# A decoder layer in one kernel: the second product of its MLP written as seven block products

## The chip, the cores and the metric

The kernel runs on one core of a Trainium2 chip. The core has TensorE (PE in the profile, with its weight loads as PEld), VectorE (DVE), ScalarE (ACT), GpSimd (POOL) and SyncE (SP), which here only starts transfers; 16 DMA engines carry those. The metric is the time of one execution on the device, in microseconds; lower is better. Times before and after are medians of several runs, and one run more is taken with the hardware profiler; the rows of this document are from that one.

## The reference, cut to what matters

One layer, for 1024 tokens of width 1024, all in fp32 (DFF is 4096):

```python
h = rmsnorm(x, norm_mix_g)
u = h @ w_in                                   # then two token mixers and two gates
x = x + merged @ w_out                         # "out_proj" below
h = rmsnorm(x, norm_mlp_g)
x = x + jnp.square(jax.nn.relu(h @ w_ff1)) @ w_ff2      # first and second product of the MLP
gate = jax.nn.sigmoid(rmsnorm(x, norm_ple_g) @ w_ple_gate)
x = x + (p @ w_ple) * gate                     # "gate stage" below
return rmsnorm(x, final_norm_g)
```

w_ff1 is 1024x4096, w_ff2 4096x1024, w_ple_gate 1024x1024.

## The kernel before, in words

**A product.** An fp32 operand is held as two parts of TensorE's faster fp32 type: a high part, which ScalarE casts, and a low part (the operand less its high part), which VectorE or GpSimd subtracts. One product of a 128x128 block with a 128x512 block is then three matmuls, hi·hi, hi·lo and lo·hi (`mm3`, L155 to L160). They accumulate in a bank of PSUM.

**The stages.** After the mixers comes `out_proj` (L882). For each half c of the output columns and each tile j of 128 tokens it makes 24 matmuls. In the second half it also runs `norm(j - 1)` behind tile j: the norm of the token tile, its transposition on TensorE (`pt`), the product with the norm's weights (`h`, L902) and, for odd j, four subtractions that prepare the operands of the MLP's first product (L907). The last tile's norm stands behind the last matmul.

`phase_ff1` (L963) makes the first product in Strassen's form. A 2x2 product of blocks takes eight block products; in this form (Winograd's variant) seven do, of sums of the blocks, and the results are sums of these. Here 16 groups of 2 column tiles of w_ff1 go through the block products ORDER = [0, 5, 1, 6, 4, 3, 2], twelve matmuls each (512 tokens wide). `stationary` (L1005) makes the weights' sums, `moving` (L993) the sums of h and their parts, once, in group 0. As these take time, products 0 and 1 of the first AHEAD = 4 groups, which need neither, are made first. The sums of the results are `u`, `v`, `x` (L1065); `store` applies the squared ReLU (L1031) and writes one 128x512 tile to `dr_hid` in DRAM (L1032), four a group.

`phase_ff2` (L1084) makes the second product in the plain way: eight groups of four rows of hidden blocks; each group loads four hidden blocks (`h0r` to `h3r`, 512 KB each) and four of w_ff2 (`w0r` to `w3r`, L1100), casts them (L952) and makes their low parts (L953), the next group's during the present one's matmuls. Each of the eight token tiles takes 24 matmuls into one tile `p` (two banks), and VectorE adds that to `x2` (L1120), which was read back from DRAM in eight loads `x` (L1110).

`phase_ple` (L1123) is the gate stage: the eight blocks of w_ple_gate are loaded and split (`plg0hi`, `plg0lo` and on; low parts on GpSimd, L1146) during the second product. Each token tile is normed (`xn`; Square on ScalarE, `rs_v`, a power on GpSimd for `rs_r`, then L122), transposed and goes through 48 matmuls for the gate (`pg`), 12 for the embedding (`pw`) and the last norm.

**What sets the order.** A scheduler of the language orders each engine's instructions by their place in the program and their readiness, before the run; on the chip every engine then works through its list in that order and waits at an instruction whose inputs are not there. SP's list holds all transfers, on one queue: a store that waits for its result holds up all the loads behind it. A tile of a pool with `bufs` buffers can be filled only when the use of the one that many before it is done.

Of the kernel before, what the change touches and what calls it, by code (L numbers as in the profile page):

```python
# [79 lines left out]
class Kern:  # L80
    def __init__(self, tc, A, out):
        self.tc, self.nc, self.A, self.out = tc, tc.nc, A, out
        self.raws = {}
# [79 lines left out]
    def run(self):  # L163
        nc, tc, A = self.nc, self.tc, self.A
        with ExitStack() as es:
# [13 lines left out]
            self.dr_hid = dr.tile([DFF // P, P, T], F32, name="dr_hid")  # L179
# [10 lines left out]
            with ExitStack() as right:  # L190
# [3 lines left out]
                self.f1w = opener(mid)("f1w", 5)  # L194
# [687 lines left out]
    def out_proj(self, pool, mA):  # L882
# [9 lines left out]
        def norm(j, xj):  # L892

            xn = self.norm_scale(xj, (nw, nw))
            nc.sync.dma_start(self.dr_x2[j, :, H:D], xj[:, H:D])
            col = lambda c: slice(c * H + j // 2 * P, c * H + (j // 2 + 1) * P)
            blk = lambda kk, c: self.h2[:, 4 * kk:4 * kk + 4, col(c)]
            for q in range(2):
# [4 lines left out]
                if j % 2 == 0:  # L903
                    self.split([t[:, :, col(0)] for t in self.hb[q]], blk(q, 0), q)
            if j % 2:
# [3 lines left out]
                sub(blk(0, 0), blk(0, 1), blk(0, 0))  # L909
                sub(t1, blk(1, 1), blk(0, 0))  # L910
                sub(blk(1, 0), blk(1, 0), t1)
                sub(blk(0, 1), blk(1, 1), blk(0, 1))

        for c in range(2):
            cols = slice(c * H, c * H + H)
            ws = [self.weights(wp, A["w_out"][k][:, cols], [P, H], "wo", lo="gv"[k % 2], raw_bufs=2) for k in range(KD)]
            for j in range(NT):
# [22 lines left out]
                if j:  # L940
# [4 lines left out]
        self.first = [self.ff1_split(self.raws[0, 0][:, 4 * i:4 * i + 4, :], i) for i in range(2)]  # L945
# [18 lines left out]

    def phase_ff1(self, pool):
# [18 lines left out]
        sums = lambda name, **k: wk.tile([P, H], F32, tag="o", name=name, **k)  # L984
        n = DFF // P // 2
# [12 lines left out]
        def stationary(g, order):  # L998
# [9 lines left out]
            for i in order:  # L1008
# [14 lines left out]
                yield i, self.ff1_split(src, g < 2 or i in (0, 1))  # L1023

        def store(g, m, c, src, on_scalar=False):

            o = sums("o")
            if on_scalar:
                nc.scalar.activation(o, src, AF.Relu)
                src = o  # L1030
            nc.vector.scalar_tensor_tensor(o, src, 0.0, src, op0=ALU.max, op1=ALU.mult)  # L1031
            nc.sync.dma_start(self.dr_hid[2 * g + m, :, c * H:c * H + H], o)  # L1032

        def product(b, i, w, first):
            for k in range(4):
                self.mm3(b, w[0][:, k, :], w[1][:, k, :], hb[i][0][:, k, :], hb[i][1][:, k, :], first and k == 0, k == 3, not first)

        p0 = {}
        for g in range(AHEAD):
            ws = self.first if g == 0 else [self.ff1_split(raws[g, 0][:, 4 * i:4 * i + 4, :], True) for i in range(2)]  # L1040
# [5 lines left out]
            bs = [PT(), PT()]  # L1046
            for i in range(2):
                product(bs[i], i, ws[i], True)
                if i == 0:
                    p0[g] = wk.tile([P, H], F32, tag=f"p0{g}", name="p0", bufs=1)  # L1050
                    nc.scalar.copy(p0[g], bs[0])
            x = sums("x00")
            nc.vector.tensor_tensor(x, p0[g], bs[1], op=ALU.add)
            store(g, 0, 0, x)
        for g in range(n):
# [203 lines left out]
```

## Time and profile before

| | before |
|---|---|
| median of 3 runs | 1812.93 us (1809.47 to 1815.6) |
| profiled execution | 1816.31 us |
| its span, first to last instruction | 1814.5 us |
| mean granted TensorE clock | 0.989 |
| PE busy | 1749.5 us (96%), 9002 matmuls |
| VectorE, ScalarE, GpSimd busy | 57%, 35%, 28% |

The span is the time from the first to the last instruction of the core. Busy shares are means over stages that have different limits, so the rows further down go stage by stage. A matmul's length in a row is from its start to its modelled end, and the next begins before that: the distance between the starts of two neighbours is what one costs. The same holds of VectorE, where the start of the next instruction counts. A bracket at a row's end is the idle time of the engine before it, and what ended it.

### The profile page before, as it was taken

How to read it: one execution, taken by the hardware profiler on the slowest of the kernel's cores; microseconds unless marked ns; L12 is line 12 of the kernel's file. 1: busy time of each engine (PE TensorE's matmuls, PEld its weight loads, DVE VectorE, ACT ScalarE, POOL GpSimd, SP SyncE). 2: the span in 40 equal slices, each digit the busy share in tenths (PEclk: the TensorE clock that was granted, in tenths of full speed). 3: DMA queues.
4: the chain of work that ended last, by engine and by line, in shares of the span. 5: the costliest groups of instructions: out<-in, count | busy, mean ns of one | idle time of the engine just before them, and what ended most of it. 6: DMA issues, size and time to landing. Idle time of an engine off the chain costs nothing. (4 is left out here: it accounts for less than half of the span.)

```text
span 1814.5 us, 24028 instructions
## 1 busy us (share of the span) xinstructions
PE 1749.5 (96%) x9002; PEld 1433.6 (79%) x9002; DVE 1028.6 (57%) x2003; ACT 626.2 (35%) x1188; POOL 502.7 (28%) x377
## 2 busy tenths in 40 slices
PE   7999999999999999999999999999999999999998
PEld 7778777777777887788787778888878888888787
DVE  6257575667656652867646896666633333332653
ACT  4231442253253252867323422222231111112432
POOL 4221122122213121101512133333355333334000
PEclk9999999999999999999999999999999999999999
DMA  4323312311222327851553233333284222203101
GB/s 163 88 70 107 91 59 77 87 47 53 73 71 85 93 77 192 249 158 48 185 177 106 91 129 121 110 108 107 93 308 162 93 93 93 93 24 116 47 36 47
DMA packets 98276, 191.66 MB, mean 106 GB/s; under 512 B 34032, under 2 KB 35056, under 8 KB 98160
## 3 DMA queue, kind: packets, MB, share of 16 engines
q1 hardware_dynamic: 98160, 190.13, 32.6%
q8 instruction: 71, 1.16, 0.3%
q14 instruction: 45, 0.37, 0.1%
HBM read 138.19 MB, written 51.90 MB: 105 GB/s over the span
## 5 line engine op out<-in xcount | busy, mean ns | idle before, releaser
L158 PE MATMUL pd<-hT,w_hi 128*128 128x512 f32 (+1 forms) x688 | 276.9, 402 | 8.3 <-DVE edge L309 3.9
L160 PE MATMUL pd<-hT,w_lo 128*128 128x512 f32 (+1 forms) x688 | 270.9, 394 | 0.3 <-DVE w_lo L152 0.3
L159 PE MATMUL pd<-hT,w_hi 128*128 128x512 f32 (+1 forms) x688 | 271.0, 394 | 0.0
L1120 DVE TENSOR_TENSOR x<-x,p 128x1024 f32<-128x1024 f32 x64 | 78.2, 1221 | 209.1 <-PE p L160 209.1
L152 POOL TENSOR_TENSOR w_lo<-w_raw,w_hi 128x1024 fp32r<-128x1024 f32 x40 | 97.1, 2428 | 294.5 <-ACT w_hi L151 294.5
L158 PEld LDWEIGHTS pd<-hT,w_hi 128*128 128x128 f32 x688 | 131.1, 191 | 34.7 <-issue 5.5
L160 PEld LDWEIGHTS pd<-hT,w_lo 128*128 128x128 f32 x688 | 131.0, 190 | 24.7 <-DVE w_lo L152 0.5
L159 PEld LDWEIGHTS pd<-hT,w_hi 128*128 128x128 f32 x688 | 131.1, 191 | 23.8 <-issue 1.4
L953 POOL TENSOR_TENSOR wlo<-s,whi 128x512 fp32r<-128x512 f32 x56 | 74.9, 1340 | 186.3 <-ACT whi L952 186.3
L952 ACT CAST whi<-s 128x512 fp32r<-128x512 f32 x64 | 39.5, 622 | 120.9 <-PE p L159 101.8
L151 ACT CAST w_hi<-w_raw 128x1024 fp32r<-128x1024 f32 x42 | 44.1, 1050 | 92.7 <-PE pd L159 82.2
L952 ACT CAST h0hi<-h0r 128x1024 fp32r<-128x1024 f32 x8 | 8.4, 1053 | 190.3 <-PE p L159 181.4
L525 DVE TENSOR_TENSOR XT<-X,LB 64x31 f32<-64x31 f32 (+15 forms) x124 | 53.6, 432 | 22.2 <-DMA LB<-dr_blk 18.3
L839 DVE CUSTOM_DVE_ANT_0 sc<-ps,tab 128x512 f32<-128x512 f32 (+3 forms) x96 | 50.6, 551 | 25.4 <-PE ps L837 24.9
L953 POOL TENSOR_TENSOR h0lo<-h0r,h0hi 128x1024 fp32r<-128x1024 f32 x8 | 19.3, 2414 | 159.8 <-ACT h0hi L952 159.8
L1031 DVE SCALAR_TENSOR_TENSOR o<-x 128x512 f32<-128x512 f32 x52 | 61.9, 1190 | 0.7
L306 DVE SCALAR_TENSOR_TENSOR mix<-pd,prm,mix 128x511 f32<-128x511 f32 x28 | 20.9, 747 | 69.2 <-ACT mix L305 69.0
L877 POOL TENSOR_TENSOR r<-e,mhalf 128x1 f32<-128x1 f32 x32 | 19.8, 620 | 140.3 <-DVE e L875 131.0
L952 ACT CAST whi<-w_raw 128x512 fp32r<-128x512 f32 x48 | 29.7, 623 | 83.0 <-PE p L159 77.9
L107 POOL TENSOR_TENSOR rs_r<-rs_v,mhalf 128x1 f32<-128x1 f32 (+1 forms) x32 | 28.9, 903 | 91.8 <-DVE rs_v L105 91.8
L526 DVE TENSOR_TENSOR X<-X,XT 64x31 f32<-64x31 f32 (+15 forms) x124 | 52.0, 419 | 4.1
L848 ACT ACTIVATE sc<-sc,nm 128x128 f32<-128x128 f32 (+7 forms) x64 | 49.5, 776 | 11.8 <-DVE nm L846 7.2
(416 smaller groups left out, 4699.5 us busy)
## 6 DMA issues: line engine op xcount, KB each, us to landing
w_raw<-w_in SPq DMA_DIRECT2D x42, 512.0 KB, 3.4
w_raw<-w_ff SPq DMA_DIRECT2D x36, 512.0 KB, 3.8
dr_hid<-o SPq DMA_DIRECT2D x64, 256.0 KB, 2.1
dr_gate<-st SPq DMA_DIRECT2D x32, 256.0 KB, 2.3
gate<-dr_gate SPq DMA_DIRECT2D x32, 256.0 KB, 2.8
xj<-x SPq DMA_DIRECT2D x8, 512.0 KB, 6.1
qs<-dr_q SPq DMA_DIRECT2D x8, 512.0 KB, 8.2
kh<-dr_k SPq DMA_DIRECT2D x16, 256.0 KB, 9.1
```

What stands on the lines that cost most here:

```text
L152: (nc.gpsimd if lo == "g" else nc.vector).tensor_tensor(lo_, raw, hi_.bitcast(F32), op=ALU.subtract)
L158: mm(out, wh, hh, start=first, stop=False, skip_group_check=more)
L159: mm(out, wh, hl, start=False, stop=False, skip_group_check=more)
L160: mm(out, wl, hh, start=False, stop=last, skip_group_check=more)
L525: nc.vector.tensor_tensor(t, X[:, 0:n, s:s + 1].to_broadcast([64, n, m]), LB[:, s:s + 1, s + 1:].to_broadcast([64, n, m]), op=ALU.mult)
L526: nc.vector.tensor_tensor(X[:, 0:n, s + 1:], X[:, 0:n, s + 1:], t, op=ALU.add)
L839: nc.vector.tensor_tensor_reduce(s[:, c0:c1], pss[:, 0:c1 - c0], tab[:, o + c0:o + c1], 1.0, NEG, op0=ALU.add, op1=ALU.max, accum_out=mx[: ...
L848: nc.scalar.activation(s[:, 0:kend], s[:, 0:kend], AF.Exp, bias=nm, scale=SLOPES[h], accum_out=t)
L952: self.nc.scalar.copy(hi, src)
L953: (self.nc.vector if on_vector else self.nc.gpsimd).tensor_tensor(lo, src, hi.bitcast(F32), op=ALU.subtract)
L1031: nc.vector.scalar_tensor_tensor(o, src, 0.0, src, op0=ALU.max, op1=ALU.mult)
L1120: nc.vector.tensor_tensor(self.x2[:, j, :], self.x2[:, j, :], pt, op=ALU.add)
```

## The change

The second product too is made in seven block products, with 2x2 blocks that are even and odd hidden blocks by halves of the tokens, and even and odd hidden blocks by halves of the output columns.

1. **The first product stores what the second needs.** Each group now ends with seven tiles in `dr_hid` (shape 7 x 16 x 128 x 512) in place of four: the four squared results and three sums of them, made by four further operations on VectorE. `relu2` is the squared ReLU, two operations on ScalarE for two of the four results, one on VectorE for the others. All low parts are made on VectorE. In the first three groups the tile `a00` is read back from DRAM (AHEAD is 3).
2. **The second product** runs in 28 steps: four groups of eight hidden blocks, seven block products each, 48 matmuls a step. `operands(step)` loads one hidden operand `h` of 1 MB from `dr_hid` (L1164) and, once a group, four blocks `b` of w_ff2 of 1 MB (L1153), makes the weights' sums on VectorE (16 subtractions a group, L1156), and casts and splits both, four pieces of 128x512 each, the next step's during the present one. Each step ends in four additions of a bank of PSUM to `x2` or to `U` (L1204).
3. **out_proj** makes the square of a norm in two halves; the four subtractions of a pair of token tiles come one tile later; tile 6's norm is in the midst of the last tile's matmuls, and products 0 and 1 of group 0 of the first product (`ahead(0)`) stand ahead of the last tile's norm. The low parts of w_out's second half are all made on VectorE.
4. **The gate stage** makes the low parts of w_ple_gate on VectorE (L1233), has three buffers for the raw blocks, the two loads of p and `xn` together, and goes through the odd token tiles first.

```diff
@@ out_proj @@
-        self.first = [self.ff1_split(self.raws[0, 0][:, 4 * i:4 * i + 4, :], i) for i in range(2)]
+        ws = [self.ff1_split(self.raws[0, 0][:, 4 * i:4 * i + 4, :], True) for i in range(2)]
+        self.ff1_load(1)
+        self.ahead(0, ws, [pd.tile([P, H], F32, tag="pd", name="po") for i in range(2)], xp.tile([P, H], F32, tag="xh", name="x00"))
         norm(NT - 1, last)
...
+    def relu2(self, o, src, on_scalar=False):
+        nc = self.nc
+        if on_scalar:
+            nc.scalar.activation(o, src, AF.Relu)
+            nc.scalar.activation(o, o, AF.Square)
+        else:
+            nc.vector.scalar_tensor_tensor(o, src, 0.0, src, op0=ALU.max, op1=ALU.mult)
+        return o
...
+    def ahead(self, g, ws, bs, x, pool=None):
+        nc = self.nc
+        for i in range(2):
+            self.product(bs[i], i, ws[i], True)
+            if i == 0:
+                p0 = self.p0[g] = (pool or self.f1w).tile([P, H], F32, tag=f"p0{g}", name="p0", bufs=1)
+                nc.scalar.copy(p0, bs[0])
+        nc.vector.tensor_tensor(x, p0, bs[1], op=ALU.add)
+        nc.sync.dma_start(self.dr_hid[0, g], self.relu2(x, x))
@@ phase_ff1 @@
-        AHEAD = 4
+        AHEAD = 3
...
-                    store(g, 0, 1, plus("x01", sb["u"], b))
+                    x = plus("a01", sb["u"], b)
+                    a[0, 1] = self.relu2(x, x)
+                    s2 = sums("s2")
+                    sub(s2, a[0, 0], x)
+                    store(6, s2)
+                    nc.vector.tensor_tensor(x, x, a[1, 1], op=ALU.add)
+                    store(4, x)
+                    sub(a[0, 0], x, a[0, 0])
+                    store(5, a[0, 0])
+                    sub(a[1, 0], a[1, 0], a[0, 0])
+                    store(2, a[1, 0])
@@ phase_ff2 @@
+        wr, hr = pool("f2w", 7), pool("f2h", 2)
+        ops = [pool(f"f2o{i}", 1) for i in range(2)]
...
+            g, i = step // 7, ORDER[step % 7]
+            if i == 0:
+                block(g, 0, 0)
+            h = hr.tile([P, KB, H], F32, tag="h", name="h")
+            nc.sync.dma_start(h, self.dr_hid[i, KB * g:KB * (g + 1)].rearrange("q p t -> p q t"))
+            if i == 0:
+                for f, c in ((0, 1), (1, 1), (1, 0)):
+                    block(g, f, c)
...
+            for q in range(KB):
+                if i == 5:
+                    sub(tmp["t0"], b01, b00, q)
+                    sub(src, b11, tmp["t0"], q)
+                elif i == 6:
+                    sub(b01, b11, b01, q)
+                elif i == 3:
+                    sub(b10, b10, tmp["t1"], q)
+                self.split([t[:, q, :] for t in mp], src[:, q, :], True)
+                self.split([t[:, q, :] for t in sp], h[:, q, :], True)
...
+        for step in range(7 * n):
+            g, i = step // 7, ORDER[step % 7]
+            (sp, mp), nxt = nxt, operands(step + 1) if step + 1 < 7 * n else None
...
+                for q in range(KB):
+                    self.mm3(b, sp[0][:, q, tok], sp[1][:, q, tok], mp[0][:, q, :], mp[1][:, q, :], share is None and q == 0, q == KB - 1, share is not None)
...
+                to = {0: u, 5: u, 1: x2(p, 0, 0), 6: x2(p, 1, 1), 4: x2(p, 1, 1), 3: x2(p, 1, 0), 2: x2(p, 0, 1)}[i]
+                nc.vector.tensor_tensor(to, to, b, op=ALU.add)
@@ phase_ple @@
-            nc.gpsimd.tensor_tensor(lo, w, hi.bitcast(F32), op=ALU.subtract)
+            nc.vector.tensor_tensor(lo, w, hi.bitcast(F32), op=ALU.subtract)
...
+        order = [*range(1, NT, 2), *range(0, NT, 2)]
+        nxt = normed(order[0])
```

SP's list from the end of the first product into the start of the second, before; `dr_hid<-o` are stores, `x` the loads of x2, `h3r` and `w3r` the last operands of the first group:

```order
L1032 DMA dr_hid<-o 128x512
L1110 DMA x_11813<-dr_x_70 128x1024
L1032 DMA dr_hid<-o 128x512
L1100 DMA h3r<-dr_hid 128x1024
L1100 DMA w3r<-w_ff 128x1024
L1110 DMA x_11813<-dr_x_70 128x1024 x7
L1100 DMA h0r<-dr_hid 128x1024
```

The same place after; `b` are blocks of w_ff2, `h` the hidden operand of a step:

```order
L1153 DMA b_11976<-w_ff 128x4x512
L1085 DMA dr_hid<-s_11937 128x512
L1085 DMA dr_hid<-a_11934 128x512
L1085 DMA dr_hid<-a_11849 128x512
L1085 DMA dr_hid<-a_11911 128x512
L1164 DMA h<-dr_hid 128x4x512
L1153 DMA b_11980<-w_ff 128x4x512
L1153 DMA b_11982<-w_ff 128x4x512
L1153 DMA b_11984<-w_ff 128x4x512
L1188 DMA x_11956<-dr_x_70 128x1024 x8
L1164 DMA h<-dr_hid 128x4x512 x2
```

Before, all but the fourth pair of the first group's operands stand ahead of the last stores. After, the first step's `h` stands behind the last four stores, and the second step's behind three blocks of w_ff2 and all eight loads of `x`.

VectorE's list in the midst of the second product, after (there is no such place before); `slo` and `mlo` are low parts of a step's two operands, `p` a bank of PSUM:

```order
L1204 TENSOR_TENSOR u<-u,p_12684 128x512
L1204 TENSOR_TENSOR u<-u,p_12698 128x512
L1156 TENSOR_TENSOR b_12500<-b_12500,t_12581 128x512 x3
L1204 TENSOR_TENSOR u<-u,p_12712 128x512
L1156 TENSOR_TENSOR b_12500<-b_12500,t_12581 128x512
L1204 TENSOR_TENSOR u<-u,p_12726 128x512
L971 TENSOR_TENSOR slo<-h,shi 128x512
L971 TENSOR_TENSOR mlo<-b_12496,mhi 128x512 x2
L971 TENSOR_TENSOR slo<-h,shi 128x512
L971 TENSOR_TENSOR mlo<-b_12496,mhi 128x512
L971 TENSOR_TENSOR slo<-h,shi 128x512
L971 TENSOR_TENSOR mlo<-b_12496,mhi 128x512
```

The additions of a step's four banks stand ahead of the low parts of the step after the next one, which so begin when the step's last matmuls are done.

GpSimd's list at the start of the gate stage, before:

```order
L1146 TENSOR_TENSOR plg5lo<-plg_raw,plg5hi 128x1024
L1146 TENSOR_TENSOR plg6lo<-plg_raw,plg6hi 128x1024
L1146 TENSOR_TENSOR plg7lo<-plg_raw,plg7hi 128x1024
L107 TENSOR_TENSOR rs_r<-rs_v,mhalf 128x1 x5
```

VectorE's list at that place, after; `x_11956` is x2:

```order
L1233 TENSOR_TENSOR plg4lo<-plg_raw,plg4hi 128x1024
L1233 TENSOR_TENSOR plg5lo<-plg_raw,plg5hi 128x1024
L1204 TENSOR_TENSOR x_11956<-x_11956,p_14068 128x512
L1233 TENSOR_TENSOR plg6lo<-plg_raw,plg6hi 128x1024
L1204 TENSOR_TENSOR x_11956<-x_11956,p_14082 128x512
L1233 TENSOR_TENSOR plg7lo<-plg_raw,plg7hi 128x1024
L1204 TENSOR_TENSOR x_11956<-x_11956,p_14096 128x512
L105 TENSOR_SCALAR rs_v<-nrm_ss 128x1
L122 TENSOR_SCALAR xn<-x_11956,rs_r 128x1024
```

The low parts of w_ple_gate have moved from GpSimd to VectorE, between the last additions of the second product and ahead of the first `rs_v` of the stage.

## Rows read from the trace of the kernel before

**Rows 1.** The page's first part: each engine's busy time, share of the span, instructions.
```profile
PE 1749.5 (96%) x9002; PEld 1433.6 (79%) x9002; DVE 1028.6 (57%) x2003; ACT 626.2 (35%) x1188; POOL 502.7 (28%) x377
```
**Rows 2.** Products: us, busy of PE PEld DVE ACT POOL, clock, DMA share, GB/s.
```profile
1022.33:1331.39 309.06, 307.39 (x1346) 253.05 (x1344) 216.78 (x277) 94.39 (x159) 101.96 (x73) 0.99 0.34 115
1331.39:1684.49 353.10, 350.34 (x1537) 289.51 (x1537) 116.81 (x83) 69.67 (x70) 142.41 (x55) 1.00 0.33 117
```
**Rows 3.** Timeline of TensorE, end of the second product (start, length, instruction).
```profile
1671.11 0.39 PE L159 MATMUL p<-w0lo,h0hi 128*128 128x512 f32 x1
...
1684.26 0.39 PE L160 MATMUL p<-w3hi,h3lo 128*128 128x512 f32 x1
```
**Rows 4.** Timeline of all engines, from the first into the second product.
```profile
1331.16 0.39 PE L160 MATMUL p<-hb2hi,wlo 128*128 128x512 f32 x1
...
1332.42 1.17 PE L158 MATMUL p<-w0hi,h0hi 128*128 128x512 f32 x4 [0.87 <-DVE x L1065]
...
1333.60 0.32 SPq L1032 DMA_DIRECT2D dr_hid<-o  x1
...
1334.01 0.38 SPq L1100 DMA_DIRECT2D h3r<-dr_hid  x1
...
1338.63 1.05 ACT L952 CAST h3hi<-h3r 128x1024 fp32r<-128x1024 f32 x1 [3.75 <-DMA h3r<-dr_hid]
...
1339.33 0.50 PE L159 MATMUL p<-w2lo,h2hi 128*128 128x512 f32 x1 [1.89 <-POOL w2lo L953]
...
1340.26 0.63 PE L160 MATMUL p<-w2hi,h2lo 128*128 128x512 f32 x1
...
1341.41 0.32 SPq L1100 DMA_DIRECT2D h0r<-dr_hid  x1
...
1343.24 0.46 PE L159 MATMUL p<-w1lo,h1hi 128*128 128x512 f32 x1
...
1351.36 1.06 ACT L952 CAST h0hi<-h0r 128x1024 fp32r<-128x1024 f32 x1 [8.88 <-DMA h0r<-dr_hid]
```
**Rows 5.** A stretch of these loads, columns as in rows 2.
```profile
1342.00:1346.00 4.00, 4.00 (x16) 3.24 (x15) 1.23 (x1) 0.47 (x1) 0.12 (x1) 0.83 1.02 417
```
**Rows 6.** Timeline of VectorE, early in the first product, GpSimd idle.
```profile
1030.00 0.68 DVE L1053 TENSOR_TENSOR x<-p,p 128x512 f32<-128x512 f32 x1
...
1036.02 0.68 DVE L953 TENSOR_TENSOR wlo<-s,whi 128x512 fp32r<-128x512 f32 x1
```
**Rows 7.** Groups of instructions of VectorE and ScalarE, first product (busy, mean ns).
```profile
L1031 DVE SCALAR_TENSOR_TENSOR o<-x 128x512 f32<-128x512 f32 x51 | 60.6, 1188 | 0.7
L952 ACT CAST whi<-s 128x512 fp32r<-128x512 f32 x64 | 39.5, 622 | 120.9 <-PE p L159 101.8 <-DVE s L1005 19.1
```
**Rows 8.** Timeline of TensorE, from out_proj into the first product.
```profile
1015.66 1.04 PE L99 MATMUL pt<-cs,nrm_xn 128*128 128x128 f32 x8
...
1020.74 1.94 PE L99 MATMUL pt<-cs,nrm_xn 128*128 128x128 f32 x8 [4.04 <-DVE nrm_xn L122]
...
1022.33 0.78 PE L158 MATMUL p<-hb0hi,whi 128*128 128x512 f32 x1
...
1025.89 0.42 PE L160 MATMUL p<-hb0hi,wlo 128*128 128x512 f32 x1
```
**Rows 9.** What TensorE waited for, 800 to 1026: total, times, longest.
```profile
PE pt L99 <- DVE nrm_xn L122: 5.9, 3, 4.0
PE po L159 <- POOL wo_lo L152: 1.4, 1, 1.4
```
**Rows 10.** Timeline of all engines, into the gate stage.
```profile
1684.49 1.03 PE L99 MATMUL pt<-cs,xn 128*128 128x128 f32 x8
1685.56 1.06 ACT L120 ACTIVATE xn<-x 128x1024 f32<-128x1024 f32 x1 [20.53 <-PE pt L99]
...
1687.83 0.75 DVE L122 TENSOR_SCALAR xn<-x,rs_r 128x1024 f32<-128x1024 f32 x1 [0.67 <-POOL rs_r L107]
...
1688.51 0.50 PE L158 MATMUL pg<-plg0hi,h 128*128 128x512 f32 x1 [0.69 <-ACT h L140]
```

More of the change, by code (lines that the diff above doesn't have):

```diff
@@ L928, in out_proj @@
                     self.mm3(po, mh[:, k, :], ml[:, k, :], ws[k][0], ws[k][1], k == 0, k == KD - 1)
+                    if (c, j, k) == (1, NT - 1, KD // 2):
+                        norm(j - 1, last)
                 if c == 0:
@@ L963, in ff1_split, with product @@
         return w
+    def relu2(self, o, src, on_scalar=False):
[3 more added lines that the diff above has]
+            nc.scalar.activation(o, o, AF.Square)
+        else:
+            nc.vector.scalar_tensor_tensor(o, src, 0.0, src, op0=ALU.max, op1=ALU.mult)
+        return o
+    def product(self, b, i, w, first):
+        hi, lo = self.hb[i]
+        for k in range(4):
+            self.mm3(b, w[0][:, k, :], w[1][:, k, :], hi[:, k, :], lo[:, k, :], first and k == 0, k == 3, not first)
+    def ahead(self, g, ws, bs, x, pool=None):
[7 more added lines that the diff above has]
+        nc.sync.dma_start(self.dr_hid[0, g], self.relu2(x, x))
     def phase_ff1(self, pool):
         nc, A = self.nc, self.A
-        hp, w1, wk = pool("f1h", 1), pool("f1s", 4), pool("f1k", 6)
+        hp, w1, wk = pool("f1h", 1), pool("f1s", 4), pool("f1k", 9)
         ps = pool("f1p", 8, space=PSUM)
@@ L1022, in stationary @@
                     src = add("s3", r(1, 0), tmp["s1"], ALU.subtract)
[L1023 to L1040, printed above, removed]
+                yield i, self.ff1_split(src, True)
+        for g in range(1, AHEAD):
+            ws = [self.ff1_split(raws[g, 0][:, 4 * i:4 * i + 4, :], True) for i in range(2)]
             if g + 1 < AHEAD:
@@ L1045, in phase_ff1 @@
                     self.ff1_load(0, m)
[L1046 to L1054, printed above, removed]
+            self.ahead(g, ws, [PT(), PT()], sums("x00"), wk)
         for g in range(n):
@@ L1072, in phase_ff1 @@
                 b = banks[i] = PT() if first else banks[{1: 0, 3: 6, 2: 4}[i]]
-                product(b, i, w, first)
+                self.product(b, i, w, first)
                 if i == 0:
@@ L1079, in phase_ff1 @@
                 elif i == 1:
-                    store(g, 0, 0, b, True)
+                    a[0, 0] = self.relu2(sums("a00"), b, True)
+                    store(0, a[0, 0])
                 elif i == 6:
@@ L1090, in phase_ff2 @@
     def phase_ff2(self, pool):
         nc, A = self.nc, self.A
-        G = 4
-        raw, ops = pool("f2r", 3), [pool(f"f2g{g}", 1) for g in range(2)]
-        p2 = pool("f2p", 4, space=PSUM)
-        def part(p, src, tag, v):
-            r = raw.tile([P, D], F32, tag=tag[0] + "r", name=tag + "r")
-            nc.sync.dma_start(r, src)
-            parts = [p.tile([P, D], F32R, tag=f"{tag}{n}", name=f"{tag}{n}") for n in ("hi", "lo")]
-            self.split(parts, r, v)
-            return parts
@@ L1105, in phase_ff2 @@
-        n = DFF // P // G
-        load = lambda g: [(part(ops[g % 2], self.dr_hid[G * g + i], f"h{i}", False), part(ops[g % 2], A["w_ff2"][G * g + i], f"w{i}", i % 2))
-                          for i in range(G)]
-        nxt = load(0)
+        KB = 4
+        n = DFF // P // 2 // KB
+        U = pool("f2u", 1).tile([P, NT // 2, H], F32, name="u")
+        wr, hr = pool("f2w", 7), pool("f2h", 2)
+        ops = [pool(f"f2o{i}", 1) for i in range(2)]
+        ps = pool("f2p", 4, space=PSUM)
+        ORDER = [0, 5, 1, 6, 4, 3, 2]
@@ L1109, in phase_ff2 @@
+        nxt = operands(0)
         for j in range(NT):
             nc.sync.dma_start(self.x2[:, j, :], self.dr_x2[j])
[L1111 to L1120 removed]
+        banks = {}
@@ L1132, in phase_ple @@
         pw = pool("plpw", 2, space=PSUM)
-        raw = lambda name, *shape: nk.tile([P, *shape], F32, tag="raw", name=name, bufs=3)
+        raw = lambda name, *shape: rp.tile([P, *shape], F32, tag="raw", name=name)
         def normed(j):
```

110 lines of the change are left out of this document (72 added, 38 removed).

## Prediction

> **What bounds the kernel now.** I read the page's busy times first: TensorE works 96% of the span, no other engine over 57% [rows 1]. The view by stage comes next: in both MLP products TensorE is busy all the time at a granted clock of 0.99 and more, while VectorE has 117 of 353 us in the second and GpSimd 142 [rows 2]. So TensorE sets the end of both, and fewer matmuls there is time saved, as long as the others keep up. Then the timeline gives the price of a matmul: 58 of them lie between 1671.11 and 1684.26, so 13.15 / 58 = 0.2267 us each [rows 3]. Last I read the seams between stages, where TensorE waits and its clock falls: into the first product [rows 8], the second [rows 4] and the gate stage [rows 10].
>
> **A. The matmuls.** The second product has 1536 now (8 groups x 8 tiles x 24) and 28 x 48 = 1344 after: 192 fewer, x 0.2267 = **-43.5 us**. The first product's number stays.
>
> **B. In between, does the work on operands stay hidden?** A group of seven steps is 336 matmuls, 76.2 us. VectorE has per group 7 x (8 low parts + 4 additions) + 16 subtractions = 100 operations of 128x512. Where it works without a gap and GpSimd rests, ten take 1030.00 to 1036.02, 0.60 us each [rows 6]: 60 us a group, hidden. In a single step the list lets the low parts begin only when the step before is done; the worst steps hold 12 to 18 operations, 7.2 to 10.8 us of a step's 10.9. That is close but never over. ScalarE casts 8 pieces of 0.62 us [rows 7], 5 us a step. Transfers are 11.5 MB a group, about 150 GB/s, where 417 was moved [rows 5]. I take 0. Not below; above, see the first rival.
>
> **C. The start of the second product.** Before, it took 353.1 us for 348.2 us of matmuls: 4.9 lost [rows 2]. They are two waits, 0.87 and 1.89, and a stretch at the lower clock level (seven starts from 1340.26 to 1343.24, 0.43 us apart; the granted clock was 0.83 at that time), about 1.8 us [rows 4, 5]. After, count from the end of the first product's last matmul. VectorE has six operations to do (sum, square, four for the stored sums), 0.2 + 3.6 us; the last store, and then `h` of step 0, which SP may not start before, go out at 4.3 (before: store 1333.60, next load 1334.01). `h3r`, half as large, was cast 4.6 us after its issue [rows 4]; with 1 MB I take 4.9, so it lands at 9.2, and TensorE starts at 10.0 at the lower level: +1.8, as before. Step 0 ends at 10.0 + 1.8 + 10.9 = 22.7. The `h` of step 1 stands behind three blocks of w_ff2 and eight loads of `x`: with itself 8.4 MB after step 0's, at 417 GB/s 20.1 us, so 29.3; cast and low part put TensorE's start at 30.3. That is 7.6 us of waiting, and 1.8 again for the clock. Lost 21.2, against 4.9: **+16.3**. Low bound: if the transfers of `x` do not delay step 1, 11.8 - 4.9 = +6.9. High: ten loads of 0.52 MB took from 1334.01 to 1351.36, 302 GB/s, with gaps in their issue [rows 4]; at that rate step 1 comes 7.7 us later, +24.
>
> The Trainium skill's "DMA: Bandwidth & Descriptors", section "Specifications", gives one core a limit of about 358 GB/s at the memory; by it the 8.4 MB take 23.4 us, an estimate, and the time would be 3.3 us more than mine. The trace moved 417 [rows 5], so the sum goes by that.
>
> **D. The start of the first product.** Before, 315.7 us from the last matmul of out_proj to the first product's end (1015.66 to 1331.39), for 1344 x 0.2267 = 304.7 and two sets of eight transposes, 1.04 each: 9.0 lost. The largest parts: 4.04 us of waiting for the last norm, and matmuls 0.445 us apart behind it (eight from 1022.33 to 1025.89) [rows 8]. After, 24 matmuls (5.4 us) cover the norm, so both go. But the sums and parts of h, 24 operations on VectorE, lose cover: two groups of products made ahead are left behind the norm, not four. VectorE's list has 53 operations from out_proj's last sum to the last part that product 2 of group 0 needs: 52 x 0.60 + 1.74 = 33 us, about 3 for the norm's own chain (Square to the end of `xn` took 1685.56 to 1688.58 in the gate stage [rows 10]) and 2 for other gaps: 38. TensorE has 120 matmuls and the transposes before that product and reaches the piece in question at 31.7. So 6.3 lost, and 1.4 elsewhere: 7.7 against 9.0, **-1.3**. Bounds: -7 if nothing waits, +6 if VectorE's operations lie as badly as some did (below). A later group has 22 operations on VectorE, four of them for the stored sums: 13 us of the 19 that its 84 matmuls take, so these are hidden.
>
> **E. out_proj.** The waits for the norm were 5.9 us in three, 4.0 of them counted in D; one for a low part from GpSimd was 1.4 [rows 9]. The split norm, tile 6's norm in the midst, and VectorE for these parts should take 1.5 of the 3.3: **-1.5** (0 to -3.3).
>
> **F. The gate stage's start.** Before, the first tile's `xn` was ready in time: transposes started at 1684.49 and the first `pg` at 1688.51 [rows 10]. After, that tile's norm is late: VectorE's list has the last low part of w_ple_gate and the last addition ahead of `rs_v`, and `xn` needs the raw buffer that this low part frees. From there Square to `xn` takes about 3 us [rows 10], and the transposes start some 3.5 late, with part of the lower clock (about 1.5): **+5**. Bounds 0 (the scheduler's tile is ready) and +9 (raw weights, three buffers in a row, come late).
>
> **Sum.** -43.5 + 16.3 - 1.3 - 1.5 + 5.0 = -25.0. The profiled execution took 1816.3, so 1791.3. It was 3.4 above the median of 1812.93, so my forecast against that median is 1788.
>
> **Rivals.**
> 1. *VectorE sets the pace of the second product* (slower). Its operations take twice as long in places of this trace: 51 of L1031 had a mean of 1.19 us, where the stretch above has 0.68 [rows 6, 7]. If they stay long without GpSimd, a group needs more than 76.2 us from 0.76 us each; the change's gain of 25 is gone at (76.2 + 6.3) / 100 = 0.82, and at 1.0 the four groups cost +95: 1883. For it: L1031's mean. Against: the long ones lie where GpSimd works on low parts (102 us in this stage [rows 2]), and after it does none there; ten in a row at 0.60 had ScalarE, TensorE and transfers beside them. Chance 0.05. The Trainium skill ("SBUF — State Buffer", section "Who interferes with whom") has GpSimd as the only engine that shares ports with VectorE; the rows agree.
> 2. *Step 1 is not held up.* Its `h` lands while step 0 runs, because the queue's loads are served side by side. The 7.6 + 1.8 go: 1778.5. For it: early loads of several tiles overlap; against: `h0r`, issued at 1341.41 behind seven loads of `x`, was cast only at 1351.36 [rows 4], 512 KB after 9.95 us. Chance 0.2.
> 3. *The start of the first product and the gate stage lie at their upper bounds*: +7.3 and +4, 1799. For it: VectorE's list is full there, and each wait on it is TensorE's. Against: the counts in D already hold gaps. Chance 0.17.
> 4. *The steps of the second product lose a little each*, as VectorE's 16 to 18 operations of a step with subtractions go over: three such steps a group, 2 us each, +24: 1812, which is no change. Chance 0.06.
>
> **How the numbers follow.** My forecast has 0.52, the rivals 0.05, 0.2, 0.17 and 0.06. About 0.3%, or 5.4 us, is what a measurement can tell from no change: under 1807.5 is faster, over 1818.4 slower. The first two cases of the change's own sign and the third are faster: 0.89; the fourth is same: 0.06; the first rival is slower: 0.05. The range goes from a little below rival 2 to a little above rival 3: 1775 to 1804. It leaves out rival 1, rival 4 and the tails.
>
> **What would show it.** The second product should have 1344 matmuls at 0.227 us; between its first and last but for steps 0 and 1 no waits over 0.5 us. At its start: TensorE's first matmul 10 us after the first product's last, ended by the cast of `h`; step 1's first, 7 to 8 us after step 0's end, again behind a transfer. In the first product one wait of some 6 us for `hb2lo` or its neighbours, none for `nrm_xn` ahead of it. In the gate stage the first transposes 3 to 4 us late, behind `xn` on VectorE. VectorE's 128x512 operations in the second product should be 0.6 us apart. The prediction is wrong if these operations take 0.8 or more, if waits recur in each group of seven steps, or if C's loads go at another rate than 417 GB/s.

## The result, and the profile after

The change makes the kernel faster: a median of 1791.72 us (1791.26 to 1794.06, four runs) against 1811.96 us of the kernel before (four runs), a ratio of 0.9892 with a 95% interval of 0.9879 to 0.9904. Measured again beside later kernels it was 1794.32 against 1811.85, a ratio of 0.9895 (0.9879 to 0.9911). That is some 20 us saved; the forecast was 25. The profiled execution took 1791.26 us, its span is 1789.3.

The page's first part after the change, which answers to [rows 1]:

```profile
PE 1707.1 (95%) x8810; PEld 1397.9 (78%) x8810; DVE 1194.1 (67%) x2456; ACT 715.2 (40%) x1414; POOL 253.1 (14%) x246
```

TensorE has 192 instructions less, VectorE 453 more, and GpSimd half the busy time. By stage (us, then busy time of PE, PEld, DVE, ACT, POOL, granted clock, DMA share, GB/s): the first product from the last matmul of out_proj on, the second product, the gate stage. They answer to [rows 2].

```profile
1009.15:1325.03 315.88, 310.44 (x1353) 253.27 (x1352) 238.25 (x380) 121.01 (x205) 1.82 (x2) 0.99 0.40 143
1325.03:1654.59 329.56, 310.04 (x1345) 255.52 (x1344) 261.79 (x420) 130.29 (x236) 0.00 (x0) 0.97 0.47 172
1654.59:1789.30 134.71, 122.85 (x585) 102.05 (x584) 71.28 (x132) 49.19 (x97) 10.71 (x16) 0.95 0.13 47
```

The second product went from 353.1 to 329.6 us. With 1344 matmuls of 0.2267 us, 304.7, it now loses 24.9 us, where the kernel before lost 4.9. Its steady part keeps that price: 796 matmuls in 180 us.

```profile
1365.00:1545.00 180.00, 180.00 (x796) 149.05 (x795) 140.90 (x231) 68.39 (x128) 0.00 (x0) 1.00 0.48 173
```

What TensorE waited for at its start stands in two rows of the timeline, with SP's issues around them (start, length, instruction, and in brackets the idle time before it and what ended it); they answer to [rows 4]:

```profile
1324.80 0.39 PE L160 MATMUL p<-hb2hi,wlo 128*128 128x512 f32 x1
1324.97 0.39 SPq L1153 DMA_DIRECT2D b<-w_ff  x1
...
1328.17 1.83 SPq L1085 DMA_DIRECT2D dr_hid<-a  x3
...
1330.05 0.45 SPq L1164 DMA_DIRECT2D h<-dr_hid  x1
1330.55 2.45 SPq L1153 DMA_DIRECT2D b<-w_ff  x3
...
1333.10 12.24 SPq L1188 DMA_DIRECT2D x<-dr_x  x8
1337.32 2.18 ACT L970 CAST shi<-h 128x512 fp32r<-128x512 f32 x4 [4.49 <-DMA h<-dr_hid]
...
1337.99 0.80 PE L158 MATMUL p<-mhi,shi 128*128 128x512 f32 x1 [12.80 <-ACT shi L970]
...
1339.01 0.63 PE L160 MATMUL p<-mhi,slo 128*128 128x512 f32 x1
1339.43 0.63 PE L158 MATMUL p<-mhi,shi 128*128 128x512 f32 x1
...
1346.26 1.63 SPq L1164 DMA_DIRECT2D h<-dr_hid  x2
...
1357.58 2.18 ACT L970 CAST shi<-h 128x512 fp32r<-128x512 f32 x4 [3.35 <-DMA h<-dr_hid]
...
1358.24 0.80 PE L158 MATMUL p<-mhi,shi 128*128 128x512 f32 x1 [6.71 <-ACT shi L970]
```

Read it from the top: the last store leaves SP at 1330, only then `h` of step 0, which is cast 7.3 us later; TensorE has then stood for 12.80 us and goes on with matmuls 0.43 us apart: the granted clock is 0.50 there, the lower level. The `h` of step 1 is issued at 1346.26, behind the eight loads of `x`, whose issue alone took 12.24 us, and TensorE stands again, for 6.71 us. After step 1 the view of TensorE's waits is empty for the rest of the product (1365 to 1655).

The 16 DMA engines were busy all that time (their share is about 1), but they moved 350 GB/s in the first wait, where stores were under way too, and over 410 later. Three stretches (columns as above), which answer to [rows 5]:

```profile
1330.00:1334.00 4.00, 0.00 (x0) 0.00 (x0) 2.50 (x4) 2.18 (x4) 0.00 (x0) 0.50 1.01 350
...
1338.00:1342.00 4.00, 4.00 (x10) 3.09 (x11) 4.00 (x7) 1.50 (x3) 0.00 (x0) 0.50 1.06 411
...
1346.00:1350.00 4.00, 4.00 (x19) 3.31 (x18) 2.73 (x5) 1.90 (x4) 0.00 (x0) 1.00 1.03 421
```

SP's queue delivers here in the order of issue. The last of the four stores lands at 1333.2, `h` of step 0 at 1337.3, the three blocks of w_ff2 2.5 to 2.6 us apart after it, the eight loads of `x` 1.2 to 1.3 us apart, and `h` of step 1 at 1357.6, 2.6 us after the last of them.

In the gate stage's first microseconds, the chain that the forecast named, to be read beside [rows 10]:

```profile
1654.60 1.23 DVE L1233 TENSOR_TENSOR plg7lo<-plg_raw,plg7hi 128x1024 fp32r<-128x1024 f32 x1 [0.87 <-ACT plg7hi L1232]
...
1655.92 1.06 ACT L120 ACTIVATE xn<-x 128x1024 f32<-128x1024 f32 x1 [1.35 <-DVE plg7lo L1233]
...
1657.99 0.75 DVE L122 TENSOR_SCALAR xn<-x,rs_r 128x1024 f32<-128x1024 f32 x1 [0.73 <-POOL rs_r L107]
1658.80 1.97 PE L99 MATMUL pt<-cs,xn 128*128 128x128 f32 x8 [4.05 <-DVE xn L122]
```

`plg7lo` is the last low part of w_ple_gate. The Square writes into the raw buffer which that operation has just freed, and the transposes start 4.05 us late.

### The profile page after: what moved, and what is told of

It is laid out like the page before. It is cut to its first block, busy times and chain, and to the rows that moved or that the text cites. A ratio compares the mean times of both kernels' runs of the same rounds, so it can differ in the third digit from the quotient of the medians.

```text
span 1789.3 us, 24058 instructions
## 1 busy us (share of the span) xinstructions
PE 1707.1 (95%) x8810; PEld 1397.9 (78%) x8810; DVE 1194.1 (67%) x2456; ACT 715.2 (40%) x1414; POOL 253.1 (14%) x246
## 4 chain that ended last, share of the span: by engine, by line
PE 51%; DVE 7%; DMA 4%; ACT 2%; issue 2%; POOL 1%; SPq 0%; POOLq 0%; DVEq 0%; ACTq 0%
PE p L158 10%; PE p L160 10%; PE p L159 10%; PE pd L159 2%; PE pd L158 2%; PE pd L160 2%; PE pg L158 1%; PE pg L160 1%; PE pg L159 1%; PE pt L99 1%; PE pt L869 1%; PE po L159 1%; PE po L160 1%; PE po L158 1%; DMA wo_raw<-w_out 1%
## 5 line engine op out<-in xcount | busy, mean ns | idle before, releaser
L158 PE MATMUL p<-mhi,shi 128*128 128x512 f32 x448 | 176.5, 394 | 19.5 <-ACT shi L970 19.5
L159 PE MATMUL p<-mlo,shi 128*128 128x512 f32 x448 | 176.2, 393 | 0.0
L160 PE MATMUL p<-mhi,slo 128*128 128x512 f32 x448 | 176.0, 393 | 0.0
L970 ACT CAST shi<-h 128x512 fp32r<-128x512 f32 x112 | 68.5, 619 | 176.1 <-PE p L159 161.3
L107 POOL TENSOR_TENSOR rs_r<-rs_v,mhalf 128x1 f32<-128x1 f32 (+1 forms) x24 | 21.9, 916 | 683.7 <-DVE rs_v L105 683.7
L158 PEld LDWEIGHTS p<-mhi,shi 128*128 128x128 f32 x448 | 85.4, 191 | 37.9 <-ACT shi L970 20.4
L160 PEld LDWEIGHTS p<-mhi,slo 128*128 128x128 f32 x448 | 85.1, 190 | 18.3 <-DVE slo L971 0.5
L159 PEld LDWEIGHTS p<-mlo,shi 128*128 128x128 f32 x448 | 85.2, 190 | 17.8
L971 DVE TENSOR_TENSOR slo<-h,shi 128x512 fp32r<-128x512 f32 x112 | 76.3, 688 | 4.9 <-ACT shi L970 4.8
L1204 DVE TENSOR_TENSOR x<-x,p 128x512 f32<-128x512 f32 x80 | 53.2, 686 | 35.0 <-PE p L160 34.8
L306 DVE SCALAR_TENSOR_TENSOR mix<-pd,prm,mix 128x511 f32<-128x511 f32 x28 | 20.9, 746 | 69.6 <-ACT mix L305 69.4
```

The lines of the kernel that those rows point to most:

```text
L107: nc.gpsimd.tensor_tensor(r, v, self.mhalf[:, :n], op=ALU.pow)
L158: mm(out, wh, hh, start=first, stop=False, skip_group_check=more)
L159: mm(out, wh, hl, start=False, stop=False, skip_group_check=more)
L160: mm(out, wl, hh, start=False, stop=last, skip_group_check=more)
L306: nc.vector.scalar_tensor_tensor(dst[:, lo + 1:lo + H], pt[:, 0:H - 1], mu, dst[:, lo + 1:lo + H], op0=ALU.mult, op1=ALU.add)
L970: self.nc.scalar.copy(hi, src)
```

## The experiments

Each kernel ran beside the kernel before, five rounds. As the parts of the change stand in different stages, I judge each edit by its stage's length in the profile first (the same instructions elsewhere vary by up to some 4 us between executions: out_proj's first matmul starts at 915.6 us in the profile of before, and at 911.4 to 915.0 in those of the changed kernels, with the same 5090 matmuls ahead of it), and by the ratio second. The lengths run from the start of one stage's last matmul to that of the next one's (the gate stage's to the end of the span).

| kernel | median us | ratio to before (95%) | first product | second product | gate stage |
|---|---|---|---|---|---|
| before | 1811.96 | 1 | 315.7 | 353.1 | 130.2 |
| changed | 1791.72 | 0.9892 (0.9879 to 0.9904) | 315.9 | 329.6 | 134.9 |
| e1, x after step 1 | 1788.16 | 0.9854 (0.9837 to 0.9871) | 314.3 | 324.7 | 134.4 |
| e2, h from ScalarE | 1789.96 | 0.9870 (0.9857 to 0.9884) | 314.3 | 329.1 | 135.2 |
| e3, xn's own buffers | 1786.87 | 0.9849 (0.9836 to 0.9863) | 315.8 | 329.5 | 128.0 |
| e4, norm first | 1791.45 | 0.9875 (0.9856 to 0.9893) | 313.8 | 329.6 | 134.5 |
| e5, changed again | 1794.32 | 0.9895 (0.9879 to 0.9911) | 314.3 | 329.7 | 133.4 |
| e6, early loads, x in quarters | 1781.48 | 0.9833 (0.9816 to 0.9850) | 314.3 | 320.8 | 132.7 |
| e7, low parts on GpSimd | 1795.39 | 0.9904 (0.9888 to 0.9919) | 314.3 | 331.0 | 136.6 |
| e8, e6 and e3 | 1776.03 | 0.9804 (0.9785 to 0.9823) | 314.3 | 319.9 | 127.8 |
| e9, four groups ahead | 1786.64 | 0.9851 (0.9836 to 0.9866) | 312.8 | 329.3 | 133.3 |
| e10, all of it | 1775.36 | 0.9790 (0.9773 to 0.9807) | 315.2 | 319.4 | 128.2 |

e1 to e4 are one series, e5 to e8 a second, e9 and e10 a third; a median is compared with another only inside its series. In the first series the kernel before had 1814.75 and the changed kernel did not run, so there the ratios are weak evidence beside the stages: e2, which forecast and stage both put near no gain, has a ratio 0.002 under the changed kernel's.

**e1: the loads of x behind step 1's operand.**

```diff
         nxt = operands(0)
-        for j in range(NT):
-            nc.sync.dma_start(self.x2[:, j, :], self.dr_x2[j])
...
             (sp, mp), nxt = nxt, operands(step + 1) if step + 1 < 7 * n else None
+            if step == 0:
+                for j in range(NT):
+                    nc.sync.dma_start(self.x2[:, j, :], self.dr_x2[j])
```

> The eight loads of x (4.2 MB) go onto SP's queue behind the hidden operand of step 1, not ahead of it. Theory (bytes in the queue): behind step 0's operand then stand 3.15 MB of w_ff2 and step 1's own 1.05 MB, at 414 GB/s 10.1 us, so it lands before step 0 has ended; the wait of 6.7 us at step 1 goes, and with it the stretch at the lower clock level, some 2.5 us: about 9 us faster than the changed kernel (1783). Rival (the operand itself is slow to come, whatever is queued ahead of it): wait and time stay, within 1 us.

The wait at step 1 went, as the theory said, but 4.9 us came of it, not 9: `h` of step 2 now stands behind the 4.2 MB of `x`, and TensorE waits there.

```profile
1339.34 0.80 PE L158 MATMUL p<-mhi,shi 128*128 128x512 f32 x1 [12.52 <-ACT shi L970]
...
1366.17 0.50 PE L158 MATMUL p<-mhi,shi 128*128 128x512 f32 x1 [2.79 <-ACT shi L970]
```

So the bytes in the queue hold up whatever comes behind them. I had not counted who stands behind `x` once it is moved.

**e2: step 0's operand and first block issued by ScalarE.**

```diff
-            nc.sync.dma_start(h, self.dr_hid[i, KB * g:KB * (g + 1)].rearrange("q p t -> p q t"))
+            (nc.sync if step else nc.scalar).dma_start(h, self.dr_hid[i, KB * g:KB * (g + 1)].rearrange("q p t -> p q t"))
```

(and the same for block b00)

> The first operand h and the first block of w_ff2 are issued by ScalarE, so that they do not stand behind SP's last four stores; nothing else is moved. Theory: the two waits at the start are one stream of 11.5 MB; h of step 0 goes out some 5 us sooner and the first wait shrinks from 12.8 to 7 or 8 us, but step 1's operand still comes when the stream has passed, so the second wait grows by about as much: 0 to 2 us faster in all (1790 to 1792). Rival (two waits, each with its own cause): 5 to 6 us faster (1786).

The theory held: `h` was issued at 1326.42, 0.6 us before the first product's end and not 5.0 after it, yet it was cast only at 1337.51, 11.1 us later. The first wait shrank to 10.99 us, the second grew to 8.47, and their sum stayed at 19.5 (20.9 in e5, the changed kernel's second profile).

```profile
1326.42 0.51 ACTq L1164 DMA_DIRECT2D h<-dr_hid  x1
1326.96 0.39 SPq L1153 DMA_DIRECT2D b<-w_ff  x1
...
1337.51 2.18 ACT L970 CAST shi<-h 128x512 fp32r<-128x512 f32 x4 [3.82 <-DMA h<-dr_hid]
```

ScalarE's transfers run on a queue of their own. On it the block b00 (1 MB) stood ahead of `h` and landed at 1331.4; after that `h` had to share the DMA engines with a store and the next block `b` on SP's queue. From 1332 to 1335 each of the two queues moved half of the bytes (packets, MB, share of the 16 engines; q10 is ScalarE's):

```profile
q1 hardware_dynamic: 298, 0.61, 54.6%
q10 hardware_dynamic: 301, 0.62, 53.1%
```

An earlier place in a full stream buys little; bytes must leave the stream, or the stream must start earlier.

**e3: buffers of its own for xn.**

```diff
-        wg, rp = pool("plg", 1), rpool("plr", 3)
+        wg, rp, xp = pool("plg", 1), rpool("plr", 4), rpool("plx", 2)
...
-            self.norm_turn(self.norm_scale(self.x2[:, j, :], (nk, nk), raw("xn", D)), "norm_ple_g", h, (nk, nk, ps))
+            self.norm_turn(self.norm_scale(self.x2[:, j, :], (nk, nk), xp.tile([P, D], F32, tag="xn", name="xn")), "norm_ple_g", h, (nk, nk, ps))
```

> xn of the gate stage gets two buffers of its own, and the raw blocks of w_ple_gate and p four, so that the first tile's norm need not wait for the last low part of w_ple_gate. Theory: the norm of tile 1 is done during the last step, the wait of 4.1 us before the first transposes goes, and most of the stretch at the lower clock level behind it (about 2): 4 to 6 us faster than the changed kernel (1786 to 1788). Rival: the first pg then waits for the last weights' parts, or the clock falls all the same: 0 to 1.5 us faster.

The gate stage went from 134.9 (133.4 in e5) to 128.0 us, as expected or a little better, and is now shorter than in the kernel before (130.2). The transposes start at once and the first `pg` follows 2.8 us later; compare the first row with the one at 1658.80 above, and with [rows 10]. The edit also gives the raw blocks and p a fourth buffer. In its trace the first tile's Square starts at 1645.49, and `plg7lo` only at 1653.29, so the norm no longer waits for that operation; whether four shared buffers alone would have done was not tried.

```profile
1656.35 1.03 PE L99 MATMUL pt<-cs,xn 128*128 128x128 f32 x8
...
1659.18 0.50 PE L158 MATMUL pg<-plg0hi,h 128*128 128x512 f32 x1
```

**e4: the last norm written ahead of `ahead(0)`.**

```diff
         self.ff1_load(1)
+        norm(NT - 1, last)
         self.ahead(0, ws, ...)
-        norm(NT - 1, last)
```

> The last tile's norm goes back ahead of the two products made early for group 0 (that one edit of the change undone). Theory of the prediction (VectorE is the narrow place at the first product's start): TensorE waits about 4 us for the norm as in the kernel before, but the later waits for parts of h and weights (about 4.6 us in the changed kernel) shrink, since VectorE gains that time: 1 to 2.5 us slower (1793 to 1794). Rival (the norm's wait is paid in full, with the lower clock behind it): 5 to 6 us slower (1797).

Neither came true, and the run tells nothing of the norm: the scheduler still put 14 of the 24 matmuls first, since the norm was not ready, and so moved the eight transposes ahead by ten matmuls only. The first product's stretch was 313.8 us, within 0.5 of e5's. What the change's order saves there could not be taken back by an edit of the program's order.

**e5: the changed kernel again**, to compare e6 to e8 with.

> The changed kernel again, with no edit, as the one that the others of this series are compared with. Its times should lie 1.0 to 1.2% under the kernel before on the same chip, and its waits where they were: 12.8 and 6.7 us at the start of the second product, 4.1 before the gate stage's first transposes.

Its time was as expected, its waits were not all where they had been: 12.5 and 8.3 us at the start of the second product, and 3.0, not 4.1, before the gate stage's first transposes. So differences of 1 to 1.5 us in the gate stage mean little.

```profile
1359.46 0.79 PE L158 MATMUL p<-mhi,shi 128*128 128x512 f32 x1 [8.34 <-ACT shi L970]
...
1658.03 1.09 PE L99 MATMUL pt<-cs,xn 128*128 128x128 f32 x8 [2.96 <-DVE xn L122]
```

Its first product is 1.6 us shorter than in the first profile of the same kernel, because there matmuls were 0.43 us apart from 1050.07 to 1053.00 (granted clock 0.51) and here they were not (1.00).

**e6: the first group's loads early, x in quarters.**

```diff
-            nc.sync.dma_start(t, A["w_ff2"][...])
+            (nc.sync if g else nc.gpsimd).dma_start(t, A["w_ff2"][...])
...
-            nc.sync.dma_start(h, self.dr_hid[...])
+            (nc.sync if step else nc.gpsimd).dma_start(h, self.dr_hid[...])
...
-        for j in range(NT):
-            nc.sync.dma_start(self.x2[:, j, :], self.dr_x2[j])
...
+            if step in (1, 2, 4, 5):
+                t, c = {1: (0, 0), 2: (1, 1), 4: (1, 0), 5: (0, 1)}[step]
+                for p in range(NT // 2):
+                    nc.sync.dma_start(x2(p, t, c), self.dr_x2[2 * p + t, :, c * H:c * H + H])
```

> Step 0's operand and the first group's four blocks of w_ff2 are issued by GpSimd, which has nothing else to do there, so that they go out before the first product ends and stand behind no store; x is loaded in quarters, two steps or so before each is added to. Theory (all that is late at the seam is late for its place on SP's queue and for the bytes in one stream): the first wait falls from 12.8 to under 2 us, the second from 6.7 to under 2, the lower clock's stretches with them; from the end of the first product to the end of the second 308 to 312 us, not 329.6: about 19 us faster than the changed kernel. Rival (the transfers themselves are slow at that point, or the queue of GpSimd is): half of that or less.

12.8 us faster than e5 by the medians (1781.48 against 1794.32); the profiled executions, from which the stages are read, are 8.8 apart. The second product is 8.9 shorter, half of what the theory said. The transfers did what it said (GpSimd issued `h` at 1317.09, nine microseconds before the first product's end, and the first wait fell to 1.98 us), but VectorE then was late:

```profile
1317.09 0.76 POOL L1164 DMA_DIRECT2D h<-dr_hid  x1
...
1328.30 0.50 PE L158 MATMUL p<-mhi,shi 128*128 128x512 f32 x1 [1.98 <-ACT shi L970]
...
1332.16 0.69 DVE L1031 TENSOR_TENSOR a<-a,a 128x512 f32<-128x512 f32 x1 [2.15 <-DMA dr_hid<-a]
1332.76 2.49 DVE L971 TENSOR_TENSOR mlo<-b,mhi 128x512 fp32r<-128x512 f32 x4
...
1333.50 0.79 PE L159 MATMUL p<-mlo,shi 128*128 128x512 f32 x1 [4.70 <-DVE mlo L971]
```

The six operations of the first product's end stand ahead of the low parts in its list, and the last of them overwrites `a10` and so waits 2.15 us for that tile's store. Neither mattered while the transfer was later still.

**e7: the hidden operand's low parts on GpSimd.**

```diff
-                self.split([t[:, q, :] for t in sp], h[:, q, :], True)
+                self.split([t[:, q, :] for t in sp], h[:, q, :], False)
```

> In the second product the low parts of the hidden operand (four of 128x512 a step) go from VectorE to GpSimd. Theory behind the forecast's first rival (VectorE's operations get longer while GpSimd works on the same kind of operand): VectorE has 72 operations a group, not 100, but those beside GpSimd's 5.4 us a step take 1.2 us or more, so their mean rises from 0.69 to over 0.85; time between 0 and 10 us slower than the changed kernel. Rival (the engines don't disturb each other): mean stays at 0.69, VectorE's load falls by a quarter, time unchanged.

VectorE and GpSimd in the steady part of the second product: first the stretch from 1380 to 1620 (columns as above), then groups from 1365 to 1640 (busy us, mean ns), of the changed kernel:

```profile
1380.00:1620.00 240.00, 240.00 (x1061) 198.72 (x1060) 197.18 (x323) 94.04 (x176) 0.00 (x0) 1.00 0.39 140
...
L971 DVE TENSOR_TENSOR slo<-h,shi 128x512 fp32r<-128x512 f32 x100 | 68.8, 688 | 0.0
L1204 DVE TENSOR_TENSOR x<-x,p 128x512 f32<-128x512 f32 x74 | 49.1, 686 | 34.7 <-PE p L160 34.7
L971 DVE TENSOR_TENSOR mlo<-b,mhi 128x512 fp32r<-128x512 f32 x72 | 48.2, 688 | 0.8 <-ACT mhi L970 0.8
```

and of e7:

```profile
1380.00:1620.00 240.00, 239.81 (x1058) 198.22 (x1057) 215.82 (x229) 93.96 (x176) 140.26 (x89) 1.00 0.41 142
...
L971 DVE TENSOR_TENSOR mlo<-b,mhi 128x512 fp32r<-128x512 f32 x71 | 90.9, 1316 | 2.4 <-ACT mhi L970 2.4
L1204 DVE TENSOR_TENSOR x<-x,p 128x512 f32<-128x512 f32 x72 | 48.1, 679 | 15.3 <-PE p L160 14.8
...
L971 POOL TENSOR_TENSOR slo<-h,shi 128x512 fp32r<-128x512 f32 x104 | 162.2, 1581 | 115.2 <-ACT shi L970 115.1
```

With 28 operations a group less to do, VectorE was busy for longer: 215.8 us of 240 (1380 to 1620), against 197.2. The low parts, both of whose inputs lie in SBUF, went from 688 to 1316 ns, while the additions, of which one input is a bank of PSUM, stayed at 0.68 us. The Trainium skill says which of the two should suffer ("SBUF — State Buffer", section "Who interferes with whom": a VectorE instruction with two SBUF inputs contends with a GpSimd instruction that reads SBUF; one with at most one, outside the two-port modes, does not). The two traces agree. The kernel's time stayed (1795.4 against 1794.3), as 216 of 240 us is still hidden. So the mechanism of the forecast's first rival exists, and the change escapes it because it leaves GpSimd idle.

**e8: e6 and e3 together.**

> The early loads, x in quarters, and the buffers of its own for xn together. If the gains stand in different places and add up: 19 + 7 = 26 us faster than the changed kernel. If the lost time at one seam only moves to the next: under 20.

18.3 us faster than e5 (1776.03), not the 26 expected. The stages show no gain lost to its neighbour: the second product is 9.8 us shorter than in e5 (8.9 in e6), the gate stage 5.6 (5.4 in e3). What is missing is e6's own shortfall.

**e9: four groups made ahead.**

```diff
-        hp, w1, wk = pool("f1h", 1), pool("f1s", 4), pool("f1k", 9)
+        hp, w1, wk = pool("f1h", 1), pool("f1s", 4), pool("f1k", 8)
...
-        AHEAD = 3
+        AHEAD = 4
```

> The first product again makes products 0 and 1 of four groups ahead of the rest, as before the change (AHEAD 4; the pool of the sums has eight buffers, not nine, so that this fits). Theory (VectorE's list is what is late at the first product's start): TensorE gets 24 matmuls, 5.4 us, of further cover, VectorE four operations, 2.4 us, of further work, so of the 6 us that are lost between 1030 and 1050 in the changed kernel about 3 go, and the lower clock's stretch behind them (1.7) may go: 3 to 5 us faster than the changed kernel. Rival (the casts on ScalarE or the sums' buffers set the pace there): within 1 us, or slower.

The first product took 312.8 us against 314.3 in e5, neither of them with a stretch at the lower clock behind its waits: 1.5 us. The waits there are almost the same (4.5 us against 5.4). out_proj got 1.0 us shorter too (96.5 against 97.5, and so in e10): TensorE's wait of 0.9 us for tile 6's `nrm_xn`, which the changed kernel and e1 to e8 have, is gone. That makes 2.5 us, still short of the theory's 3 to 5. The ratio speaks for more (0.9851 against 0.9895), but the two are of different series, and the stages show no more, so I leave that open.

**e10: all of it**, and the last stored sum in a buffer of its own:

```diff
-                    sub(a[1, 0], a[1, 0], a[0, 0])
-                    store(2, a[1, 0])
+                    s10 = sums("s10")
+                    sub(s10, a[1, 0], a[0, 0])
+                    store(2, s10)
```

> Early loads, x in quarters, xn's own buffers and four groups ahead together, and the last stored sum of each group written to a buffer of its own, so that VectorE need not wait for the store of a10 (2.0 us in the last group). If each part keeps its gain: e8's gain over the changed kernel and 5 to 7 us more, 1769 to 1771 on the chip of the second series (ratio to the kernel before about 0.977).

1775.36 us, a ratio of 0.9790 to before, not the 0.977 expected. The wait for `mlo` at step 0 fell from 4.70 to 2.65 us, as expected, but the first product got 2.4 us longer than in e9. In each group product 1 now begins late, behind ScalarE's copy of product 0's bank (a weight load idle for 0.26 us, and 0.34 us instead of 0.23 between two matmuls), which neither e8 nor e9 shows:

```profile
1140.60 0.58 ACT L1103 COPY p<-p 128x512 f32<-128x512 f32 x1
...
1141.22 0.19 PEld L158 LDWEIGHTS p<-hb1hi,whi 128*128 128x128 f32 x1 [0.26 <-ACT p L1103]
1141.23 0.50 PE L158 MATMUL p<-hb1hi,whi 128*128 128x512 f32 x1
...
1141.57 0.39 PE L159 MATMUL p<-hb1lo,whi 128*128 128x512 f32 x1
```

Over the groups that is about 2 us (790 matmuls in 180 us, 1120 to 1300, against 796). As neither e8 nor e9 has it, it comes of the new buffer or of several edits together; which of them was not tried. So e10 is level with e8, whose interval overlaps. Both beat the changed kernel and the kernel before.

## Why the prediction was right, and where its size was off

The direction and the mechanisms held: 192 matmuls fewer, at a steady price, and a loss at three seams. The stages give every term of the sum.

- **A, -43.5.** In the steady parts TensorE makes 796 matmuls in 180 us before and after alike (1120 to 1300, and 1365 to 1545 in the new second product), and no wait stands between step 2 and the end of the second product. The price and the count held.
- **B, 0.** VectorE's low parts took 688 ns each, as in [rows 6], and nothing waited for them. e7 shows what the first rival would have been made of; it needs GpSimd at work.
- **C, +16.3: too small.** Measured 24.9 - 4.9 = +20.0. The first wait was 12.8 us, not 10.0: `h` went out 5.0 us after the last matmul's end, not 4.3, and landed 7.2 us after its issue, not 4.9. That 4.9 is the term that was mis-sized. I had taken the 4.6 us of a 512 KB load in [rows 4] and added 0.3 for 512 KB more, though at 417 GB/s they take 1.3; and of the four stores ahead of `h` I had counted the wait for their issue, not their bytes. The four are 1.05 MB; the last of them landed 3.1 us after `h` was issued, and `h` 4.1 us after that. In those 4.1 us the engines moved 361 GB/s, 1.5 MB, so at least 0.4 MB of it was not `h` but what stood behind it; this sharing is the smaller part. The second wait was 6.7 us against 7.6 (8.3 in e5): step 1's operand was cast 20.3 us after step 0's (1337.32 to 1357.58), against 20.1, so counting the bytes ahead at 417 GB/s was right there, where a stream of loads kept the queue full. The rest, 24.9 - 19.5 = 5.4 us, is nearly all the lower clock level at the two restarts (5.0 by the starts of the matmuls), where I had put 3.6. Those 8.4 MB in 20.3 us are 414 GB/s. The Trainium skill's "DMA: Bandwidth & Descriptors" (section "Specifications") gives about 358 as a core's limit at the memory; by it, an estimate, they would have taken 23.4 us. Here the measurement decides, and it lies above that limit.
- **Rival 2** (step 1 not held up) fell: e1 removes the wait by moving `x`, and the wait comes back at step 2. Rivals 3 and 4 fell too: D and F stayed under their upper bounds (+0.2 of +6 and +4.7 of +9), and no step after the first two lost time.
- **D, -1.3.** Measured +0.2, and -1.4 in e5. The waits are where the forecast had them, but not in one piece: from 1030 to 1050 VectorE is busy for 19.97 of 20 us and TensorE makes 56 matmuls where 88 fit, in waits of up to 1.1 us for casts of `whi` (2.8 us in four), `wlo` and `hb3lo` (0.9 each). The casts wait in their turn for VectorE's sums. One more wait, of 0.8 us, is for `hb0lo`, a low part of h that GpSimd still makes. The loss of about 7 us there is near the 6.3 worked out. That matmuls 0.43 us apart follow in one profile and not in the other is the difference of 1.6 us.
- **E, -1.5.** Measured -2.3, from out_proj's first matmul to its last (99.8 to 97.5).
- **F, +5.** Measured +4.7 (and +3.2 in e5). e3 takes the wait away by taking `xn` out of the weights' buffers, which is the cause named, though it adds a buffer for the weights too.

The four stages together make -2.3 + 0.2 - 23.5 + 4.7 = -20.9, which is the -20 of the medians. The two spans differ by 25.2, just the forecast, but 4.2 of that lie ahead of out_proj, where both kernels have the same instructions: the agreement of the spans is luck, and the sum was 4 us too hopeful, nearly all of it in C.

## What to carry to other kernels

Take matmuls away and the price is paid at the seams: of the 43.5 us saved here, 25 went to three restarts of TensorE (C and F), and in e8 some 15 of these came back (9.8 and 5.6 in the two stages, against e5) by issuing the first loads from an idle engine ahead of the stores, by loading what is needed late in pieces, and by not letting a norm share a buffer with weights. For a load at a seam, count the bytes ahead of it in its queue, those of stores too, and what another queue moves meanwhile (half of all, in e2). The sum of two waits on one stream can then be forecast better than each (19.5 us in the changed kernel and in e2, 20.9 in e5). When such a wait is removed, look at once for who is next in line: here a sum on VectorE that waited for a store.

## What the runs showed of the hardware that I had not expected

- A 1 MB load of `h` took 5.7 us from issue to landing as the median of 28, but 7.2 and 11.3 us at the start of the second product, behind other transfers in its queue, and 11.1 in e2, where a second queue took half of the bytes.
- Moving a quarter of VectorE's operations to GpSimd made VectorE's busy time longer (197 to 216 us of 240), not shorter.
- The same waits of up to 1.1 us each are followed by a stretch at the lower clock level in some executions (1050 to 1053 in the first profile of the changed kernel, granted clock 0.51, and 3 us in e3, 0.52) and not in others (e5, 1.00); it costs 1.6 us.
